# One transpose shared by two heads in the edge tiles of a neighbourhood attention

## The chip, the core and the metric

The kernel runs on one core of a Trainium2 chip. A core has five engines that work side by side, each through its own queue in order: TensorE (PE: matmuls and transposes), VectorE (DVE), ScalarE (ACT), GpSimd (POOL) and SyncE (SP, which here only issues transfers). SBUF is the on-chip memory with 128 partitions; PSUM holds the results of PE. The metric is the time of one execution on the device, in microseconds (us); smaller is better.

## What is computed

One layer of an encoder on 1024 tokens of width 1024, in float32: a projection, then a convolution group and an attention group side by side, an output projection, and a gated feed-forward block. The change concerns the attention alone: eight heads of width 64 on a grid of 16 rows by 64 columns, where each query sees a window of 8 rows by 16 columns, shifted inwards at the edges.

```python
def row_block(r):
    row_start = jnp.clip(r - kh // 2, 0, rows - kh)
    q_r = lax.dynamic_index_in_dim(qg, r, axis=1, keepdims=False)
    k_rows = lax.dynamic_slice_in_dim(kg, row_start, kh, axis=1)
    v_rows = lax.dynamic_slice_in_dim(vg, row_start, kh, axis=1)
    k_win = k_rows[:, :, col_idx]
    v_win = v_rows[:, :, col_idx]
    s = jnp.einsum("bqhd,brqchd->bhqrc", q_r, k_win) * scale
    ...
    s = s + jnp.transpose(bias, (0, 2, 1, 3))[None]
    p = jax.nn.softmax(s, axis=(-2, -1))
    return jnp.einsum("bhqrc,brqchd->bqhd", p.astype(v_win.dtype), v_win)
```

## The kernel before

The queries are cut into eight tiles of 128: `rh` is the upper or lower half of the grid rows, `cb` one of four blocks of 16 columns. A tile's keys are a rectangle: 11 or 12 grid rows (`AR`) by 23, 31, 31 or 24 grid columns (`WIN`). `order` takes the tiles as stages in the order cb = 0, 3, 1, 2, upper half before lower. The first four stages are those at the grid's left and right edge: stage 0, tile (0, 0), has 11 x 23 = 253 keys; stage 1, tile (1, 0), 12 x 23 = 276; stages 2 and 3, tiles (0, 3) and (1, 3), 12 x 24 = 288. Stages 4 to 7 have up to 12 x 31 = 372. Each stage has four head pairs, so there are 32 pairs, number `i`.

The instructions stand in the order in which the Python code is written (`manual_schedule`); each engine works its own queue in order, and waits by semaphores. The main loop runs i = 2 to 33; one turn of it is called a pass below. Pass i does, for PE: the two score matmuls of pair i (`score_mm`, tiles `s`), the transposes of pair i - 2 (`flip`, from `e` to the PSUM tile `p`), in odd passes up to 17 four transposes for the convolution (`conv_norm`, tile `y`), and the weighing of pair i - 3 (`weigh`, value matmuls into `o`). Between them DVE adds the bias table `tab` and finds the maximum, ACT takes the exponential (`score_exp`), POOL scales the row by its sum (`score_norm`), and ACT (second head, `hh` = 1) and DVE (first head) copy the transposed block from `p` into SBUF as `pT` (`flip_out`). There is one buffer for `p`, so the transposes of a pass wait for the copies of the pass before.

A pair's keys do not fit one transpose, whose result has at most 128 partitions. `parts` cuts them: 253 keys into two overlapping pieces of 125 and 128, all others by grid rows into three pieces of four rows, 92, 96 or 124 keys. A pair of stages 1 to 3 takes six transposes and six value matmuls, each of 128 output columns. In the weighing the first head goes to partitions 0 to 63 of `o`, the second to 64 to 127.

The values are written by `value_out` (ACT) to the tensor `vd` in device memory, one row of 512 floats per token with the heads in order, and read back by SP's queue in the windows that the stages need: `load_v00` for stage 0, `load_vw` for four grid rows of a column window, two of them in one SBUF tile `vw`. The bias tables are read by the same queue (`table`), and so are the weights of the output projection (`issue`). Loads and stores take eight semaphore lanes in turn, so that a load waits, besides for its data and buffer, for the one eight places ahead of it.

In the profile `p` is line 713, `pT` 718, `o` 730, `s` 682, `e` 695 (DVE), 697 (ACT) and 704 (POOL), `y` 831, `vs` 444 and its store 445, `vw` 644, `v00` 658 to 662, `tab` 632. `z` at lines 124 to 126 are matmuls of the projections before, `zt` their transposes.

Of the kernel before, what the change touches and what calls it, by code (L numbers as in the profile page):

```python
# [76 lines left out]
def build(ctx, tc, a):  # L77
# [569 lines left out]
    SPLIT = 125  # L647
    v00 = []

    def load_v00(j):  # L650
        if not v00:
            w = G("v00").rearrange("p (g d) -> p g d", d=512)
            v00.extend((w[:SPLIT, 0], w[:, 1]))
        src = vd.rearrange("(r c) d -> r c d", c=GW)
        ncol = WIN[0][1]
        r, c = divmod(SPLIT, ncol)
        if j == 0:
            nc.sync.dma_start(v00[0][:r * ncol], src[:r, :ncol, :])
            nc.sync.dma_start(v00[0][r * ncol:], src[r, :c, :])
        else:  # L660
            nc.sync.dma_start(v00[1][:ncol - c], src[r, c:ncol, :])
            nc.sync.dma_start(v00[1][ncol - c:], src[r + 1:AR[0][0], :ncol, :])

    def parts(rh, cb):
        m = 4 * WIN[cb][1]
        if rh == cb == 0:
            return [(0, P, v00[0]), (SPLIT, SPLIT + P, v00[1])]
        return [(g * m, g * m + m, vw[cb, rh + g]) for g in range(3)]

    k4 = kT.rearrange("p c (r w) -> p c r w", w=GW)  # L670
    order = [(rh, cb) for cb in (0, 3, 1, 2) for rh in range(2)]
    tab, es, pTs, os_, at, sums, pp = {}, {}, {}, {}, {}, {}, {}
# [14 lines left out]
    def score_exp(i, ss):  # L687
        s_, hp = divmod(i, 4)
        rh, cb = order[s_]
        n = AR[rh][KIND[cb]] * WIN[cb][1]  # L690
        e = es[i] = G(f"e{i}").rearrange("p (h n) -> p h n", h=2)[:, :, :n]
        rs = SM(f"rs{i}", 2)
        for hh in range(2):
            mx = SM(f"mx{i}{hh}", 1)
            dve.tensor_tensor_reduce(out=e[:, hh], in0=ss[hh], in1=tab[rh, cb][2 * hp + hh], scale=-1.0,  # L695
                                     scalar=3.0e38, op0=OP.add, op1=OP.min, accum_out=mx)
            act.activation(e[:, hh], e[:, hh], AF.Exp, bias=mx, scale=-1.0, accum_out=rs[:, hh:hh + 1])  # L697
        sums[i] = rs
# [7 lines left out]
    def flip(i):  # L706
        s_, hp = divmod(i, 4)
        cuts = parts(*order[s_])
        pp[i] = cv(f"p{i}")
        for hh in range(2):  # L710
            for g, (l, r, _) in enumerate(cuts):
                o = hh * 512 + g * P
                pe.transpose(pp[i][:r - l, o:o + P], es[i][:, hh, l:r], ident)  # L713
        pTs[i] = G(f"pT{i}").rearrange("p (n h q) -> p n h q", h=2, q=P)[:cuts[0][1], :len(cuts)]

    def flip_out(i, hh):
        m, n = pTs[i].shape[:2]
        (dve.tensor_copy, act.copy)[hh](pTs[i][:, :, hh], pp[i][:m, hh * 512:hh * 512 + n * P].rearrange(
            "p (n q) -> p n q", q=P))

    def weigh(i):
# [4 lines left out]
        cuts = parts(rh, cb)  # L726
        for g, (_, _, v) in enumerate(cuts):
            for hh in range(2):
                c = (2 * hp + hh) * HD
                pe.matmul(os_[s_][hh * HD:(hh + 1) * HD, hp], v[:, c:c + HD], pTs[i][:v.shape[0], g, hh],  # L730
                          start=g == 0, stop=g == len(cuts) - 1)
# [49 lines left out]
    for j in range(2):  # L781
        load_v00(j)
# [6 lines left out]
    for g in range(1, 4):  # L789
        load_vw(0, g)  # L790
    load_window(3)
# [648 lines left out]
```

## Time and profile before

| | |
|---|---|
| median of 3 runs | 1045.03 us (1044.88 to 1046.16) |
| the profiled execution | 1046.69 us, span of its instructions 1045.0 us |
| granted clock of PE | 0.997 |
| passes 2 to 18 of the loop | about 237 to 278 us of the span |

A profile is one execution. Its span runs from the first to the last instruction. All instants below are us from the span's start. A busy PE is not PE at its peak, since matmuls are pipelined and their ends are modelled; the chain of waits tells whether it is PE that everything waits for.

### The profile page before, as it was taken

What the parts mean: (1) busy time and instruction counts of PE and PEld (TensorE: products, weight loads), DVE (VectorE), ACT (ScalarE), POOL (GpSimd) and SP (SyncE); (2) the same over time, 40 slices, a digit from 0 to 9 for tenths busy, and PEclk for the clock granted to TensorE, in tenths of its full rate; (3) what the DMA queues carried; (4) which work ended last, traced back from release to release, by engine and by line L of the source; (5) the groups of instructions that cost most, each with busy time, mean ns of one, the idle gap of its engine ahead of it and who ended that gap; (6) DMA issues with size and microseconds to landing.
All of it is one profiled execution on the core that took longest, in us unless ns stands there. A gap on an engine that the chain in (4) does not pass through costs nothing.

```text
span 1045.0 us, 13870 instructions
## 1 busy us (share of the span) xinstructions
PE 1027.6 (98%) x4948; PEld 833.0 (80%) x4948; DVE 719.4 (69%) x1097; ACT 464.0 (44%) x915; POOL 451.9 (43%) x344
## 2 busy tenths in 40 slices
PE   7999999999999999999999999999999999999997
PEld 6888888876668888778888888888888888888886
DVE  6878998976885576876655655546556567768883
ACT  6465346627775676533232233232322443443441
POOL 0136668923574962754544454555454100002310
PEclk9999999999999999999999999999999999999999
DMA  9496871285546844555232232232232697634641
GB/s 355 169 261 232 211 226 64 78 241 180 158 106 156 171 170 148 123 143 186 84 131 101 73 132 98 99 123 101 91 111 81 212 328 254 204 101 130 212 131 41
DMA packets 73939, 162.44 MB, mean 155 GB/s; under 512 B 13533, under 2 KB 20445, under 8 KB 73166
## 3 DMA queue, kind: packets, MB, share of 16 engines
q1 hardware_dynamic: 67038, 143.64, 41.1%
q0 software_dynamic: 4864, 10.49, 6.2%
q10 hardware_dynamic: 1968, 7.42, 2.1%
q8 instruction: 39, 0.64, 0.2%
q14 instruction: 30, 0.25, 0.1%
HBM read 122.67 MB, written 52.71 MB: 168 GB/s over the span
## 4 chain that ended last, share of the span: by engine, by line
PE 91%; DVE 3%; ACT 2%; issue 2%; POOL 2%; DMA 1%; SPq 0%; POOLq 0%; ACTq 0%
PE B L125 5%; PE B L126 5%; PE B L124 5%; PE z L125 4%; PE z L124 4%; PE z L126 4%; PE D L126 4%; PE D L125 4%; PE D L124 4%; PE A L126 3%; PE A L125 3%; PE A L124 3%; PE gl L126 3%; PE gl L124 3%; PE gl L125 3%; PE n L124 3%
## 5 line engine op out<-in xcount | busy, mean ns | idle before, releaser
L358 DVE SCALAR_TENSOR_TENSOR cv<-u,par,cv 128x1009 f32<-128x1009 f32 (+14 forms) x85 | 108.5, 1276 | 1.9
L384 POOL TENSOR_TENSOR pa<-pa,pr 128x1022 f32<-128x1022 f32 (+10 forms) x31 | 75.5, 2435 | 33.2 <-ACT pr L383 32.3
L1395 POOL TENSOR_TENSOR ou<-ou,resm 128x512 f32<-128x512 f32 x8 | 12.8, 1608 | 141.3 <-DMA resm<-xd 140.7
L116 ACT CAST op<-sr 128x512 fp32r<-128x512 f32 x77 | 47.7, 619 | 53.0 <-PE B2d L126 22.1
L120 DVE TENSOR_TENSOR op<-sr,op 128x512 fp32r<-128x512 f32 x77 | 58.2, 756 | 15.8 <-ACT op L116 15.8
L1232 DVE TENSOR_TENSOR g<-B,g 128x512 f32<-128x512 f32 x22 | 15.2, 690 | 71.3 <-PE B L126 68.2
L1241 ACT ACTIVATE D<-D 128x512 f32<-128x512 f32 x22 | 12.8, 582 | 113.4 <-DVE D L1240 113.4
L1224 DVE TENSOR_TENSOR u<-B,g 128x512 f32<-128x512 f32 x22 | 15.2, 691 | 61.0 <-PE B L126 61.0
L116 ACT CAST op<-wd 128x512 fp32r<-128x512 f32 x66 | 40.9, 620 | 30.3 <-DVE wd L1319 17.1
L704 POOL TENSOR_SCALAR e<-e,rs 128x372 f32<-128x372 f32 (+3 forms) x64 | 34.6, 565 | 43.2 <-DVE rs L702 32.8
L120 DVE TENSOR_TENSOR op<-wd,op 128x512 fp32r<-128x512 f32 x66 | 51.4, 778 | 2.0 <-ACT op L116 0.3
L1025 DVE TENSOR_TENSOR ts<-ts,gu 128x512 f32<-128x512 f32 x36 | 43.3, 1203 | 0.6
L1230 ACT ACTIVATE A<-A 128x512 f32<-128x512 f32 x18 | 10.5, 582 | 68.6 <-PE A L126 68.6
L697 ACT ACTIVATE e<-e,mx 128x372 f32<-128x372 f32 (+3 forms) x64 | 35.6, 559 | 2.3 <-DVE mx L695 2.2
L695 DVE CUSTOM_DVE_ANT_0 e<-s,tab 128x372 f32<-128x372 f32 (+3 forms) x64 | 28.9, 489 | 8.6 <-PE s L682 8.1
L383 ACT ACTIVATE pr<-u,par 128x1022 f32<-128x1022 f32 (+10 forms) x31 | 34.2, 1135 | 1.2 <-ACT vs L444 1.2
L713 PEld LDWEIGHTS p<-ident,e 128*124 128x124 f32 (+3 forms) x184 | 19.2, 134 | 16.9 <-POOL e L704 9.6
L1025 DVE TENSOR_TENSOR ts<-gu 128x512 f32<-128x512 f32 x18 | 30.1, 1670 | 0.0
L903 DVE TENSOR_TENSOR x<-x,n 128x512 f32<-128x512 f32 x32 | 21.0, 681 | 13.1 <-PE n L126 13.1
L713 PE MATMUL p<-ident,e 128*124 128x128 f32 (+3 forms) x184 | 27.7, 281 | 1.7 <-POOL e L704 0.8
L682 PE MATMUL s<-kT,qT 64*128 64x372 f32 (+3 forms) x128 | 26.1, 485 | 0.0
L124 PE MATMUL B2d<-op 128*128 128x512 f32 x66 | 25.8, 391 | 0.0
(1070 smaller groups left out, 3524.0 us busy)
## 6 DMA issues: line engine op xcount, KB each, us to landing
sr<-sd SPq DMA_DIRECT2D x77, 256.0 KB
gu<-in_gu SPq DMA_DIRECT2D x36, 512.0 KB
sd<-sd SPq DMA_DIRECT2D x22, 512.0 KB
wd<-in_wd SPq DMA_DIRECT2D x44, 256.0 KB
sd<-g SPq DMA_DIRECT2D x33, 256.0 KB
x<-in_x SPq DMA_DIRECT2D x12, 512.0 KB
xd<-x SPq DMA_DIRECT2D x8, 512.0 KB
resm<-xd SPq DMA_DIRECT2D x16, 256.0 KB
```

What stands on the lines that cost most here:

```text
L116: act.copy(hi, src)
L120: eng.tensor_tensor(*[w[..., sl] for w in (lo, src, hi.bitcast(F32))], OP.subtract)
L124: pe.matmul(acc, lh, rh, start=start, stop=False, skip_group_check=True)
L125: pe.matmul(acc, lh, rl, start=False, stop=False, skip_group_check=True)
L126: pe.matmul(acc, ll, rh, start=False, stop=stop, skip_group_check=True)
L358: dve.scalar_tensor_tensor(acc[:, o], uc[:, i], dwk[:, c, t:t + 1], acc[:, o], OP.mult, OP.add)
L383: act.activation(pr[:, o], uc[:, i], AF.Copy, scale=dwk[:, c, t:t + 1])
L384: pool.tensor_tensor(pa[:, o], pa[:, o], pr[:, o], OP.add)
L697: act.activation(e[:, hh], e[:, hh], AF.Exp, bias=mx, scale=-1.0, accum_out=rs[:, hh:hh + 1])
L704: pool.tensor_scalar(es[i][:, hh], es[i][:, hh], rs[:, hh:hh + 1], 1.0, op0=OP.mult, op1=OP.mult)
L713: pe.transpose(pp[i][:r - l, o:o + P], es[i][:, hh, l:r], ident)
L1025: dve.tensor_tensor(lr(tsum[i, 1])[n - 3] if o is None else o, l, r, OP.add)
```

## The change

In stages 1 to 3 the first head's keys are cut as 128, then up to the last 32, then these 32; the second head's as the first 32, then the middle, then the last 128. The two pieces of 32 keys lie side by side in memory, since the two heads' scores now stand in `e` without a gap, and one transpose of 64 columns (`flip`, the branch `if left`) takes both. A pair has five transposes: four of 128 columns and the shared one. ACT and DVE copy two blocks each instead of three, and DVE copies the 64 x 128 block as well. `weigh` still has six matmuls; the last two contract 32 keys, one on partitions 0 to 31, the other on 32 to 63.

The pieces no longer are whole grid rows, and differ between the two heads. `load_edge` loads them by ranges of keys, for the four even and the four odd heads apart; for this `vd` now has the even heads in its first 256 columns and the odd ones in the last 256 (`value_out`). A range is one load for its whole grid rows and one for each part of a row, so an edge takes 14 loads into a tile `ve` and a short tile `vl`. The loads of stages 1 and 2 are issued ahead of the loop, in the place of the seven loads of `vw`, those of stage 3 in pass 4. Stage 0 keeps its cut (`load_corner`).

```diff
     def value_out(t, z):
         vs = ST(f"vs{t}")
-        act.activation(vs, z, AF.Copy, scale=r1[:, t:t + 1])
+        by_head = lambda w, order: w.rearrange(f"p ({order} d) -> p c h d", h=2, c=4)
+        act.activation(by_head(vs, "h c"), by_head(z, "c h"), AF.Copy, scale=r1[:, t:t + 1])
...
+    LEFT = 32
+    cuts = {}
+
+    def load_keys(dst, rh, cb, l, r, cols=slice(0, 512)):
+        c0, ncol = WIN[cb]
+        src = vd.rearrange("(r c) d -> r c d", c=GW)[4 * rh:, c0:c0 + ncol, cols]
+        at_ = l
+        while at_ < r:
+            row, c = divmod(at_, ncol)
+            n = (r - at_) // ncol if c == 0 else 0
+            end = at_ + n * ncol if n else min(r, (row + 1) * ncol)
+            nc.sync.dma_start(dst[at_ - l:end - l], src[row:row + n] if n else src[row, c:c + end - at_, :])
+            at_ = end
...
+    def load_edge(rh, cb):
+        n = AR[rh][KIND[cb]] * WIN[cb][1]
+        w = G(f"ve{rh}{cb}").rearrange("p (g d) -> p g d", d=512)
+        left = ST(f"vl{rh}{cb}")[:2 * LEFT, :256]
+        ends = ((0, P, n - LEFT), (LEFT, n - P, n))
+        for g in range(2):
+            for hh in range(2):
+                l, r = ends[hh][g:g + 2]
+                cols = slice(hh * 256, hh * 256 + 256)
+                load_keys(w[:r - l, g, cols], rh, cb, l, r, cols)
+        for hh, l in enumerate((n - LEFT, 0)):
+            load_keys(left[hh * LEFT:(hh + 1) * LEFT], rh, cb, l, l + LEFT, slice(hh * 256, hh * 256 + 256))
+        cuts[rh, cb] = [[(e[g], w[:e[g + 1] - e[g], g]) for g in range(2)] for e in ends], (n - LEFT, left)
...
-        e = es[i] = G(f"e{i}").rearrange("p (h n) -> p h n", h=2)[:, :, :n]
+        flat[i] = G(f"e{i}")[:, :2 * n]
+        e = es[i] = flat[i].rearrange("p (h n) -> p h n", h=2)
...
         for hh in range(2):
-            for g, (l, r, _) in enumerate(cuts):
+            some, left = parts(*order[s_], hh)
+            for g, (l, r, _) in enumerate(some):
                 o = hh * 512 + g * P
                 pe.transpose(pp[i][:r - l, o:o + P], es[i][:, hh, l:r], ident)
+        if left:
+            pe.transpose(pp[i][:2 * LEFT, 256:384], flat[i][:, left[0]:left[0] + 2 * LEFT], ident)
...
+        copy(pTs[i][:m, :n, hh], pp[i][:m, hh * 512:hh * 512 + n * P].rearrange("p (n q) -> p n q", q=P))
+        if left and hh == 0:
+            copy(pTs[i][:2 * LEFT, 2, 0], pp[i][:2 * LEFT, 256:384])
...
+                if left and g == 2:
+                    ks = slice(hh * LEFT, hh * LEFT + LEFT)
+                    l, r = left[1][ks, hp * HD:hp * HD + HD], pTs[i][ks, 2, 0]
+                else:
+                    v, c = both[hh][0][g][2], hh * 256 + hp * HD
+                    l, r = v[:, c:c + HD], pTs[i][:v.shape[0], g, hh]
+                pe.matmul(os_[s_][hh * HD:(hh + 1) * HD, hp], l, r, start=g == 0, stop=g == n - 1)
...
-    for g in range(1, 4):
-        load_vw(0, g)
-    load_window(3)
+    load_edge(1, 0)
+    load_edge(0, 3)
     tab[1, 3] = table(1, 2)
...
+        if i == 4:
+            load_edge(1, 3)
```

Three places in the queues show what stands where. The first is PE's queue in an odd pass, the seventh (the scores of pair 7, the transposes of pair 5, `y`, and the first weighing of stage 1). Before:

```order
L682 MATMUL s_2316<-kT,qT 128x276
L682 MATMUL s_2318<-kT,qT 128x276
L713 MATMUL p_2323<-ident,e_2255 92x128 x6
L831 MATMUL y_2341<-ident,u_557 128x128
L831 MATMUL y_2341<-ident,u_986 128x128
L831 MATMUL y_2341<-ident,u_1155 128x128
L831 MATMUL y_2341<-ident,u_1338 128x128
L730 MATMUL o_2351<-pT_2297,vw_2135 64x128 x2
L730 MATMUL o_2351<-pT_2297,vw_2137 64x128 x4
```

And after (here `s` is line 703, `p` 735, the shared transpose 737, `y` 862, `o` 764):

```order
L703 MATMUL s_2353<-kT,qT 128x276
L703 MATMUL s_2355<-kT,qT 128x276
L735 MATMUL p_2360<-ident,e_2292 128x128 x4
L737 MATMUL p_2360<-ident,e_2292 64x128
L862 MATMUL y_2378<-ident,u_557 128x128
L862 MATMUL y_2378<-ident,u_986 128x128
L862 MATMUL y_2378<-ident,u_1155 128x128
L862 MATMUL y_2378<-ident,u_1338 128x128
L764 MATMUL o_2388<-pT_2333,ve_2135 64x128 x4
L764 MATMUL o_2388<-pT_2333,vl_2136 64x128 x2
```

The single transpose of 64 rows has come to stand between those of 128 and `y`, and the last two value matmuls read `vl`. In an even pass `y` is missing, and `o` follows the shared transpose at once.

The second place is DVE's queue in the same pass. Before:

```order
L702 RECIPROCAL rs_2300<-rs_2300 128x2
L695 ISA e_2332,mx_2334<-s_2316,tab_1977 128x276
L695 ISA mx_2334 128x1
L695 ISA e_2332,mx_2337<-s_2318,tab_1977 128x276
L695 ISA mx_2337 128x1
L718 COPY pT_2330<-p_2323 92x3x128
L840 BN_STATS bs_2346<-y_2341 128x6
```

And after:

```order
L724 RECIPROCAL rs_2336<-rs_2336 128x2
L717 ISA e_2368,mx_2370<-s_2353,tab_1977 128x276
L717 ISA mx_2370 128x1
L717 ISA e_2368,mx_2373<-s_2355,tab_1977 128x276
L717 ISA mx_2373 128x1
L744 COPY pT_2366<-p_2360 128x2x128
L746 COPY pT_2366<-p_2360 64x128
L871 BN_STATS bs_2383<-y_2378 128x6
```

One copy of three blocks has become one of two blocks and one of the shared block.

The third place is SP's queue behind the loads of stage 0, with the semaphores that a row waits for (`DMAHW` with a number is one of the eight lanes of the loads, so a wait for it is one for an earlier load or store). Before, from the last two `vw` loads ahead of the loop:

```order
L644 DMA vw_2143<-vd 96x1x512 [waits DMAHW5_49,DVE_49]
L644 DMA vw_2143<-vd 96x1x512 [waits DMAHW6_49]
L632 DMA tab_2146<-tf_108 128x2304 [waits PE_49]
L160 DMA P30r<-in_w 128x1024 [waits DMAHW0_49]
L632 DMA tab_2239<-tf_104 128x2976 [waits PE_49]
L644 DMA vw_2277<-vd 124x1x512 [waits DMAHW2_49,PE_49,Pool_49]
```

And after, from the same table (`tab_2167`, for stage 3) to the middle of the third edge's loads; the table of stage 4 (`tab_2239` before, `tab_2276` after) comes eight rows later:

```order
L633 DMA tab_2167<-tf_108 128x2304 [waits DMAHW4_49,PE_49]
L160 DMA P30r<-in_w 128x1024 [waits DMAHW5_49]
L659 DMA ve_2233<-vd 120x1x256 [waits DMAHW6_49]
L659 DMA ve_2233<-vd 8x256 [waits DMAHW7_49]
L659 DMA ve_2233<-vd 16x256 [waits DMAHW0_49]
L659 DMA ve_2233<-vd 96x1x256 [waits DMAHW1_49]
L659 DMA ve_2233<-vd 16x256 [waits DMAHW2_49]
L659 DMA ve_2233<-vd 16x256 [waits DMAHW3_49]
L659 DMA ve_2233<-vd 96x1x256 [waits DMAHW4_49]
```

Between the two tables now stand the 14 loads of an edge, of which the seventh waits for the lane of the first table. Ahead of `tab_2167` stand 28 loads where seven stood.

More of the change, by code (lines that the diff above doesn't have):

```diff
@@ L665, in parts @@
+    def parts(rh, cb, hh):
         m = 4 * WIN[cb][1]
[L666 to L668 removed]
+        if (rh, cb) in cuts:
+            return [(l, l + P, v) for l, v in cuts[rh, cb][0][hh]], cuts[rh, cb][1]
+        return [(g * m, g * m + m, vw[cb, rh + g]) for g in range(3)], None
     k4 = kT.rearrange("p c (r w) -> p c r w", w=GW)
     order = [(rh, cb) for cb in (0, 3, 1, 2) for rh in range(2)]
+    flat = {}
@@ L780, in build @@
     value(6)
-    for j in range(2):
-        load_v00(j)
+    load_corner()
     score_exp(0, s0)
```

41 lines of the change are left out of this document (15 added, 26 removed).

## The prediction

> **What bounds the kernel now.** I read the page's engine row first, then the busy times of the stretch that the change touches, then the chain of waits through it, and last what the queue of SyncE (SP) and VectorE (DVE) do there.
>
> ```profile
> PE 1027.6 (98%) x4948; PEld 833.0 (80%) x4948; DVE 719.4 (69%) x1097; ACT 464.0 (44%) x915; POOL 451.9 (43%) x344
> 248.60:270.00 21.40, 21.40 (x210) 15.21 (x210) 17.09 (x66) 16.79 (x51) 9.39 (x19) 1.00 0.68 207
> 276.00:311.00 35.00, 33.76 (x296) 21.01 (x298) 30.28 (x109) 28.20 (x87) 26.27 (x42) 1.00 0.41 110
> ```
>
> The second and third rows are stretches (from:to, length, then PE, PEld, DVE, ACT, POOL busy, granted clock, DMA share, GB/s). In the first of them, which holds most of the edge stages, TensorE (PE) is busy for all of 21.40 us at a clock of 1.00. Busy is not the same as needed, so the chain of waits has the word (start, length, what; xN is the number of records, of which a plain fp32 matmul shows two and a transpose one):
>
> ```profile
> 202.09 0.44 PE zt L431 x4
> 202.53 0.23 PE z L124
> ...
> 224.34 0.63 PE s L682 x4
> 224.96 0.43 PE z L124
> 225.40 0.24 PE z L125
> ...
> 238.26 0.38 ACT pT L718
> 238.66 0.43 DVE pT L718
> ...
> 241.55 0.59 PE p L713 x4
> 242.14 0.59 PE o L730 x8
> ...
> 247.76 0.83 PE p L713 x6
> 248.59 0.44 PE y L831 x4
> 249.03 0.81 PE o L730 x12
> 249.83 0.68 PE s L682 x4
> 250.52 0.79 PE p L713 x6
> 251.31 0.81 PE o L730 x12
> ...
> 258.59 0.44 PE y L831 x4
> 259.03 0.81 PE o L730 x12
> 259.83 0.69 PE s L682 x4
> ...
> 269.84 0.82 PE s L682 x4
> ...
> 275.95 0.82 PE p L713 x6
> 276.79 0.48 ACT pT L718
> 277.27 1.18 ACT e L697 x4
> ```
>
> From 247.76 to 276.79 every piece of the chain is PE, each starting where the one before it ends. So here a microsecond of PE is a microsecond of the kernel; behind 276.79 the chain goes over ACT, DVE and POOL, started by a PE group, and hands any shift on.
>
> The same rows give two prices. Per item: p x4 takes 0.59 and p x6 0.79, o x8 (four matmuls) 0.59 and o x12 (six) 0.81, y x4 0.44. Each transpose and each 128-column matmul costs 0.10 to 0.11 us. Per group: 0.59 is not 4 x 0.11 but 0.15 more, in p and in o alike, while y, which follows p, costs 0.44 = 4 x 0.11 and nothing more. What differs is the part of the array used. The built program marks p, y and z as 128x128 (rows x columns), o as 128x64, s as 64x128. From p to y the part stays; p to o, o to s and s to p change it. The z rows say the same: after zt (128x128 too) z takes its usual 0.23, after s 0.43, that is 0.20 more. I read 0.15 to 0.20 us as the price of a change of the array's part, and take 0.15, the value of the two groups (p, o) that the change touches.
>
> **The change, part by part.** It concerns passes 6 to 18 of the attention loop: twelve head pairs of the three edge stages, six of them transposed in odd passes, where y stands behind p, and six in even ones, where o does.
>
> Removed: one transpose in each of twelve pairs, six becoming five. 12 x 0.11 = 1.3 us less on PE. The four full ones are 128 wide instead of 92 or 96; p x4 at 0.59 is that width already.
>
> Added on PE, changes of part. The shared transpose yields 64 rows, and the program marks it 128x64; the two last matmuls of each weighing contract 32 keys and are marked 32x64. In an even pass the order was s, p, o, s (three changes); now s, p, shared p, o, last o, s, where shared p and o have one part: four. In an odd pass it was s, p, y, o, s (three); now s, p, shared p, y, o, last o, s: six. Counting all matmuls of the built program gives 100 changes before and 124 after. 6 x 1 + 6 x 3 = 24, by 0.15 = 3.6 us more. The number of matmuls in a weighing stays at six, and I give the short ones the same 0.11: the two heads sit side by side in the array's columns already, so 32 rows make no new room. [...] Bounds for the changes: 24 x 0 = 0 if such short groups hide it, 24 x 0.20 = 4.8 by z behind s.
>
> Added on PE, semaphores. In the first weighing of each edge every matmul waits for its own loads, and PE's queue holds 20 more semaphore instructions than before (132 for 112).
>
> ```profile
> L713 PEldq EVENT_SEMAPHORE  x31: 51/51/51, 239.1 to 315.1; - x31
> L718 DVE COPY pT<-p 96x384 f32<-96x384 f32 x8 | 4.4, 554 | 2.2 <-ACT pT L718 2.2
> L718 ACT COPY pT<-p 96x384 f32<-96x384 f32 x8 | 3.8, 474 | 3.9 <-PE p L713 3.9
> L718 DVE COPY pT<-p 128x256 f32<-128x256 f32 x3 | 1.3, 423 | 0.1
> L718 ACT COPY pT<-p 128x256 f32<-128x256 f32 x3 | 1.1, 372 | 0.8 <-PE p L713 0.7
> ```
>
> At 51 ns they are 1.0 us at most and nothing at least, since the queue runs ahead of a 0.11 us matmul; I take 0.2.
>
> DVE and ACT. ACT's copy shrinks from 474 to 372 ns. DVE's goes from 554 to 423, and a 64x128 copy follows; by the slope (131 ns for 128 elements) it is 423 - 131 = 292. DVE gains 0.16 us per pair, 1.9 in all, against 21.40 - 17.09 = 4.3 us of free time in one stretch. Before the next p may overwrite the tile, the chain is ACT 0.37, DVE 0.42, DVE 0.29: 1.08 us, where it was 0.47 + 0.55 = 1.02. PE's time between two p of an even pass, o and s, is 0.81 + 0.69 = 1.5 and grows by a change of part. So it is covered, with 0.4 us to spare less hand-overs; were that cover gone, the 0.06 by twelve would be 0.7 us.
>
> value_out on ACT writes the same 512 columns in another order. Its store feeds loads that PE wants several us later (next part), so a slower write is hidden; its price is open, zero by its size.
>
> SP's queue. Seven loads become 42, in three groups of 14.
>
> ```profile
> 216.42 0.48 SPq L659 DMA_DIRECT2D v<-vd  x1
> 216.96 0.31 SPq L661 DMA_DIRECT2D v<-vd  x1
> 229.41 0.77 SPq L662 DMA_DIRECT2D v<-vd  x1
> 239.78 0.61 SPq L644 DMA_DIRECT2D vw<-vd  x1
> 243.25 0.56 SPq L632 DMA_DIRECT2D tab<-tf  x1
> 244.33 1.16 SPq L632 DMA_DIRECT2D tab<-tf  x1
> 245.60 17.00 SPq L644 DMA_DIRECT2D vw<-vd  x4
> 262.70 2.35 SPq L632 DMA_DIRECT2D tab<-tf  x1
> ```
>
> A 115-row load holds the queue 0.77, a 92-row one 0.61, one of 10 or 13 rows 0.31 to 0.48. A group of 14 is 2 x 0.8 + 2 x 0.6 + 10 x 0.35 = 6.3 us. The last value rows are there at 239.78 (the queue had waited for their store). Seven loads of the first edge are then left: 0.8 + 6 x 0.35 = 2.9, to 242.7, and PE wants them at 249.03. The second edge ends at 249.0, wanted at 259.03, its first weighing. The table of stage (1, 3) is then issued at 249 instead of 243.25 and wanted by DVE when s of 259.83 is done: 10 us for 1152 KB. The third edge, the next 6.3 us and some waiting, puts the table of stage 4 at about 258 instead of 244.33; it is wanted at s of 269.84, 11 us later, plus PE's own delay. The window loads behind it stood in the queue until 262.6 before, so from there the queue is level again. All of this lies beside PE: 0, with 1 to 4 us if a table is late.
>
> Sum against the profiled execution, span 1045.0, time 1046.69: -1.3 + 3.6 + 0.2 = +2.5 us, 1049.2. The three runs have a median of 1045.03, 1.66 below that execution; on their scale it is 1045.03 + 2.5 = **1047.5 us**, 0.24% slower.
>
> **Rivals.**
> (a) The change of part is not paid in groups of one or two records, because the array's latency covers it. For it: the price is known here only from groups of four or more. Against it: z after s pays it at once, in its first record. Then -1.3 + 0.2: 1043.9, not slower. It decides below 0.055 us per change (1.3 / 24).
> (b) The shared transpose runs on the full array after all. Then y and p stay together, only the change inside the weighing remains, 12 x 0.15 = 1.8, less 1.3, plus 0.2: +0.7, 1045.7. For it: the instruction only drops columns, as the 92-wide transposes did, which pay nothing before y. Against: the program's mark. [...] No row of the kernel before shows a 64-wide transpose, so the trace cannot say yet.
> (c) A table comes late. Eight loads may be under way on SP's queue (each waits for the load eight places ahead), so the third edge waits for the table and the weights in front of it. If that costs 6 us, the table of stage 4 is issued at 264, lands near 273, and DVE, ACT, POOL and PE of pass 16 stand for about 3.5 us: 1051.0. For it: that table is the last of a crowded queue and needs 1488 KB. Against: the margin of 11 us above, and DMA is 0.68 busy, not full.
> (d) The stage behind 276.79 gives some of it back, its waits being on ACT and POOL: half of 2.5 us, 1046.3. The chain hands over from PE to ACT at 276.79, which speaks against it.
>
> **How the numbers follow.** I give the forecast 0.55, (a) 0.15, (b) 0.13, (c) 0.10, (d) 0.07. The forecast's own range is 24 changes at 0.09 to 0.20 with semaphores 0 to 1.0: 1.3 less than 2.2 and 5.8, so 1045.9 to 1049.5. The range for all reaches to (a) below and a little past that above, 1043.8 to 1049.8; it leaves out (c) and a part of (a). A difference of 0.2% is 2.1 us, about what a measurement of this kernel tells from none. Of the forecast two thirds lie above it (0.37); with (c) and strays 0.49 is slower. Faster by as much needs more than the whole transpose saving: 0.06. The rest, 0.45, is the same.
>
> **What the profile after would show.** PE from the first edge transposes to pass 18 longer by 2 to 3 us; in odd passes a gap ahead of and behind the single shared transpose and ahead of the 32-key matmuls; p x4 still 0.59; no DVE row waiting for a table. Wrong: y starting 0.11 behind the shared transpose (b), the last o pair without a gap (a), or a tab wait near pass 12 or 16 (c).

## The result: 0.7% slower, and the profile after

| | before | after |
|---|---|---|
| median, six runs each | 1045.52 us (1044.88 to 1046.30) | 1053.00 us (1051.92 to 1054.75) |
| ratio | | 1.0072, 95% interval 1.0059 to 1.0084 |
| the profiled execution | 1046.69 us, span 1045.0 us | 1053.88 us, span 1052.2 us |

The loss is 7.5 us, where 2.5 were forecast and 1049.8 us was the end of the range. The engine row of the page hardly shows it (PE 1027.6 us busy before):

```profile
PE 1029.5 (98%) x4936; PEld 831.8 (79%) x4936; DVE 721.8 (69%) x1109; ACT 463.5 (44%) x915; POOL 451.6 (43%) x344
```

So the starts of the score matmuls `s` tell where the time went; each is read from the timeline of PE in both runs.

| score matmuls of pair | before | after | difference |
|---|---|---|---|
| 8 | 249.76 | 249.45 | -0.31 |
| 18 | 275.05 | 275.25 | +0.20 |
| 20 | 279.92 | 280.97 | +1.05 |
| 21 | 282.48 | 283.40 | +0.92 |
| 22 | 285.20 | 292.40 | +7.20 |
| 23 | 287.80 | 296.22 | +8.42 |
| 31 | 308.60 | 317.01 | +8.41 |

All of the edge stages, where the prediction looked for the loss, add half a microsecond. Six come in one step between pairs 21 and 22. (The span grows by 7.2, not 8.4: a run of the kernel before that is told below spent 1.0 us less behind the loop than the profiled one, so this part varies by itself. In the profiled one the granted clock fell to 0.50 once there, for 3.41 us from 448.86; in the other it didn't.)

First the half microsecond. The chain of waits in an odd and an even pass after:

```profile
247.44 0.58 PE p L735 x4
248.02 0.11 PE p L737
248.13 0.44 PE y L862 x4
248.57 0.95 PE o L764 x12
249.52 0.69 PE s L703 x4
250.21 0.58 PE p L735 x4
250.79 0.11 PE p L737
250.91 0.95 PE o L764 x12
```

The shared transpose (line 737) takes 0.11 right behind the full ones, and `y` takes its 0.44 right behind it, so no change of the array's part is paid on either side. The weighing takes 0.95 where it took 0.81.

Now the step of six. The chain of waits across it, and the timeline of PE (in brackets the idle time before an instruction, and what ended it):

```profile
267.23 14.99 DMA tab<-tf
...
282.29 5.42 issue
...
287.84 0.54 DVE e L717
```

```profile
280.60 0.44 PE L764 MATMUL o<-pT,vw 124*64 124x128 f32 x4 [0.48 <-DMA vw<-vd]
...
283.40 0.90 PE L703 MATMUL s<-kT,qT 64*128 64x372 f32 x4
289.48 1.51 PE L735 MATMUL p<-ident,e 128*124 128x128 f32 x6 [5.18 <-DVE rcq L885]
290.92 1.55 PE L764 MATMUL o<-pT,vw 124*64 124x128 f32 x12
292.40 1.61 PE L703 MATMUL s<-kT,qT 64*128 64x372 f32 x4
293.94 1.54 PE L735 MATMUL p<-ident,e 128*124 128x128 f32 x6
295.41 0.88 PE L764 MATMUL o<-pT,vw 124*64 124x128 f32 x12
296.22 0.90 PE L703 MATMUL s<-kT,qT 64*128 64x372 f32 x4
```

DVE stands from 282.3 to 287.8 before `e` of pair 20, the first of stage 5, and what it waits for is that stage's bias table, issued at 267.23. (The chain calls the last 5.42 us "issue", since no single event matches; the transfer ahead of it names the table. Its last landing in this trace is at 287.63.) The same `e` in the timeline of DVE before, without a wait:

```profile
282.01 0.53 DVE L695 CUSTOM_DVE_ANT_0 e<-s,tab 128x372 f32<-128x372 f32 x1
```

Behind that `e` on DVE stands the copy that frees the tile `p`, so PE stands too, for 5.18 us; the first weighing of stage 4 had already waited for its window `vw`. And when PE starts again, its groups take 1.5 to 1.6 us in place of 0.9 for four groups. The busy times of that stretch (length, then PE, PEld, DVE, ACT, POOL, granted clock, DMA share, GB/s) say why:

```profile
290.00:295.00 5.00, 5.00 (x26) 3.31 (x25) 3.44 (x15) 2.02 (x7) 3.66 (x6) 0.50 0.57 170
```

The granted clock is 0.50, where it was 1.00 at the same place before. Two of the four slow groups, the scores of pair 22 and the transposes behind them, make the step from +7.20 to +8.42: 1.2 us on top of the wait. The two ahead of them, of 1.51 and 1.55, are part of the step to +7.20, next to the wait of 5.18. In this trace the clock fell within the 5.18 us of idle time, at 288.55, and came back at 295.37, 5.9 us after PE had started again.

Why the table is late begins in SP's queue (start, time in the queue):

```profile
252.00 7.64 SPq L659 DMA_DIRECT2D ve<-vd  x10
259.74 1.52 SPq L659 DMA_DIRECT2D vl<-vd  x4
261.35 0.36 SPq L633 DMA_DIRECT2D tab<-tf  x1
261.75 5.38 SPq L645 DMA_DIRECT2D vw<-vd  x4
267.23 5.04 SPq L633 DMA_DIRECT2D tab<-tf  x1
```

The third edge's 14 loads take 9.3 us. Behind them come stage 4's table, the window for stages 4 and 5, and at 267.23 the table in question, which had been issued at 262.70 before. Three more rows count: the bytes moved, before and after, and the busy times of a stretch of the kernel before while that table was on its way.

```profile
DMA packets 73939, 162.44 MB, mean 155 GB/s; under 512 B 13533, under 2 KB 20445, under 8 KB 73166
```

```profile
DMA packets 75344, 162.84 MB, mean 155 GB/s; under 512 B 13893, under 2 KB 22509, under 8 KB 74570
```

```profile
274.00:285.00 11.00, 10.75 (x102) 6.94 (x101) 10.13 (x38) 9.41 (x27) 6.93 (x12) 1.00 0.26 96
```

The change moves 0.40 MB more: stages 2 and 3 used to share a set of four blocks, now each edge loads its own. And while the last of the table was on its way, the DMA engines were busy by a quarter only.

The landings recorded in the traces tell which part of the table is late. Behind its issue a load of four grid rows has four landings, a table 16. Of the table in question twelve come by 272.33 before and by 279.92 after. The last four come at 280.93 to 281.75 before and at 285.93 to 287.63 after, behind the last landing of the fourth window load (278.18 and 283.79).

### The profile page after: what moved, and what is told of

It is laid out like the page before. It is cut to its first block, busy times and chain, and to the rows that moved or that the text cites. A ratio compares the mean times of both kernels' runs of the same rounds, so it can differ in the third digit from the quotient of the medians.

```text
span 1052.2 us, 13934 instructions
## 1 busy us (share of the span) xinstructions
PE 1029.5 (98%) x4936; PEld 831.8 (79%) x4936; DVE 721.8 (69%) x1109; ACT 463.5 (44%) x915; POOL 451.6 (43%) x344
## 2 busy tenths in 40 slices
DMA packets 75344, 162.84 MB, mean 155 GB/s; under 512 B 13893, under 2 KB 22509, under 8 KB 74570
## 4 chain that ended last, share of the span: by engine, by line
PE 92%; DMA 2%; DVE 2%; issue 1%; POOL 1%; ACT 1%; SPq 0%; POOLq 0%; DVEq 0%; ACTq 0%
PE B L124 6%; PE B L125 6%; PE B L126 6%; PE z L125 4%; PE z L124 4%; PE z L126 4%; PE D L125 4%; PE A L124 4%; PE D L126 4%; PE A L125 4%; PE A L126 4%; PE D L124 4%; PE gl L124 3%; PE gl L125 3%; PE gl L126 3%; PE n L124 3%
## 5 line engine op out<-in xcount | busy, mean ns | idle before, releaser
L735 PEld LDWEIGHTS p<-ident,e 128*124 128x124 f32 (+1 forms) x160 | 17.9, 145 | 22.0 <-issue 13.5
L735 PE MATMUL p<-ident,e 128*124 128x128 f32 (+1 forms) x160 | 26.5, 295 | 6.5 <-DVE rcq L885 5.2
```

## The experiments

Theory P is the prediction's (changes of the array's part). All others start from the late table: T says that it is the loss. The other letters are guesses why it is late: the time that the 14 loads hold SP's queue (Q), their bytes (B, Y), their number (N), or four DMA engines that are full (W, F). C is about the clock. Each time is a median beside runs of the kernel before on the same chip, with the ratio to these.

### Order: the table ahead of the window

```diff
-        if i in (6, 18):
+        if i in (9, 18):
             load_window(1 + i // 18)
```

In the changed kernel:

> The changed kernel, with one edit: window 1 is loaded in pass 9, behind stage 5's bias table, where pass 6 loaded it ahead of that table. Computes the reference. Theory T (the loss is DVE's wait for stage 5's table, whose last pieces share four DMA engines with the window loads): the wait of 5.55 us ahead of e(20) goes, and with it PE's idle time of 5.2 us and the half clock behind it; what stays is the PE part, +0.5, and a wait of the first weighing of stage 4 for its window, 1 to 3 us: 1046.0 to 1049.0. Theory P (the prediction's: the changes of the array's part cost the time): nothing changes, 1052 to 1054.

And in the kernel before:

> The kernel before, with the same edit as the run above (window 1 loaded in pass 9, behind stage 5's table). Computes the reference. Theory T: the kernel before had no wait for that table, only 0.3 us to spare, so nothing is won; the window comes later, and may cost up to 2 us in the first weighing of stage 4: 1045.0 to 1047.0. It is the fair base for the run above: the difference of the two is the PE part, +0.5 by T, +2.5 by P (sum of the prediction).

The changed kernel took 1052.08 us (ratio 1.0061, 1.0047 to 1.0074), the kernel before 1045.58 (0.9996, 0.9988 to 1.0005). The first is outside T's range and inside P's. But P had said that nothing changes, and that isn't so: the table's wait is gone, and the timeline of PE shows about the same loss at the first weighing of stage 4.

```profile
279.40 0.44 PE L764 MATMUL o<-pT,vw 124*64 124x128 f32 x4 [0.46 <-DMA vw<-vd]
281.90 0.44 PE L764 MATMUL o<-pT,vw 124*64 124x128 f32 x4 [2.06 <-DMA vw<-vd]
284.41 0.69 PE L764 MATMUL o<-pT,vw 124*64 124x128 f32 x4 [2.06 <-DMA vw<-vd]
```

Each block of four grid rows (124 packets of 2 KB) comes 2.5 us after the one before. So the order only chooses who waits: table and window together are late. For the kernel before the order makes no difference. The two runs differ by 6.5 us, where T had 0.5 and P 2.5. One more thing this order shows: SP was through with the table at 264.1 here and at 272.27 in the changed kernel, so it was not the table's buffer that held the issue there.

### The loads without the change on PE

```diff
-        ends = ((0, P, n - LEFT), (LEFT, n - P, n))
...
+        blocks = [w[:m, 0], w[:m, 1], left[:m]]
...
+        cuts[rh, cb] = [[(g * m, blocks[g]) for g in range(3)]] * 2, None
```

> The changed kernel with its part on PE undone: each edge stage is again cut in three key blocks of 92 or 96 rows, six transposes and six weighings of full height per pair, no shared transpose; the loads stay three groups of 14 (in half heads), at the same places, of the same bytes. Computes the reference. Theory T: the loss is in SP's queue and stays: 1051 to 1053, with DVE waiting some 4 to 6 us for stage 5's table. Theory P: back at the kernel before, 1045 to 1046.5.

1057.04 us (1.0107, 1.0089 to 1.0126): the loss is in the loads, and P falls. (An edge takes 13 loads here, not 14, of the same bytes.) The loss is even larger than the change's, and past T's range; in the profiled run the table went out later still. From its chain of waits:

```profile
273.24 17.27 DMA tab<-tf
```


### PE kept busy during the wait

```diff
             ss = score_mm(i)
+            if i == 21:
+                for _ in range(44):
+                    pe.transpose(os_[4][:, 3], ident, ident)
```

> The changed kernel with 44 more transposes of the identity on PE (4.8 us of work nobody reads), put into the 5.2 us in which PE stood idle in pass 21 behind s(21). Computes the reference. Theory C (part of the loss is the granted clock, 0.50 for 290 to 295 us, behind that idle time): with PE kept busy the clock stays at 1.00, the groups of passes 21 and 22 take 0.87 instead of 1.55, and the kernel is faster than the changed one by 1 to 2 us, though it does more: 1051.0 to 1052.0. Rival (the slow groups hide behind DVE and ACT, which come out of the same wait): 1053 or slightly more, clock 1.00 or not.

1056.53 us (1.0101, 1.0087 to 1.0115), slower than the changed kernel, but it doesn't tell what was asked. In its profiled run the table was issued at 274.01, not 267.23, ahead of anything that the edit touches, and PE had stood 3.7 us for the window before. Why these transfers came later is open. Behind the filling the groups have the length that C said:

```profile
289.75 5.02 PE L985 MATMUL o<-ident 128*128 128x128 f32 x44
294.61 0.82 PE L735 MATMUL p<-ident,e 128*124 128x128 f32 x6
295.36 0.88 PE L764 MATMUL o<-pT,vw 124*64 124x128 f32 x12
```

0.82 and 0.88 instead of 1.5. But DVE was free again at 291.1, so that the filling itself stood in the way until 294.6.

### The third edge left out

```diff
         if i == 4:
-            load_edge(1, 3)
+            cuts[1, 3] = cuts[0, 3]
```

> The changed kernel without the 14 loads of its third edge; stage 3 is weighed with the values of stage 2's edge instead (wrong values, same work on every other engine). Everything of the change on PE, DVE and ACT stays. Theory Q (the 14 loads hold SP's queue some 9 us, so that the window's and stage 5's table's transfers start late and bunch up on the DMA engines): the window is issued near 252 and stage 5's table by about 264 as before; no wait for either, time 1045.5 to 1046.5, of which +0.5 is PE's. Theory W (it is the window loads' four DMA engines alone that are too slow, whenever they start): a wait of 2 us or more for window or table stays, 1048 to 1053.

1046.51 us (1.0007, 0.9997 to 1.0016), at the end of Q's range and below W's. Of the 7.5 us 0.9 is left. PE does all that it does in the changed kernel, and its score matmuls drift by +0.51 from pair 8 to pair 18, as they do there. SP:

```profile
252.46 2.77 SPq L645 DMA_DIRECT2D vw<-vd  x4
255.32 7.18 SPq L633 DMA_DIRECT2D tab<-tf  x1
```

This shows that the third edge's loads cost some 6.6 us, and PE's part about half a microsecond. What about them costs it is the next question. It isn't the table's issue alone: here the table went out at 255.32, 7.4 us earlier than in the kernel before, and its last landing is at 281.41, where it was 281.75.

### Each window load cut into rows

```diff
+        for r in range(4):
+            nc.sync.dma_start(vw[cb, g][r * ncol:(r + 1) * ncol], grid[g * 4 + r, c0:c0 + ncol, :])
```

> The changed kernel, with each window load of 4 grid rows cut into four loads of one row (16 for a window where there were 4). Computes the reference. [...] Theory Q: the queue is as late as before or later, with 12 more loads in it, so the table is no earlier: 1052 to 1056.

1110.68 us (1.0621, 1.0606 to 1.0635), far past Q's range. Theory W had this run faster than the changed kernel, on an estimate of the author's that a load of one row is spread over more DMA engines than one of four rows. The run shows the opposite. While PE waited for these loads, the busy times read

```profile
282.00:300.00 18.00, 1.13 (x8) 0.52 (x8) 0.00 (x0) 0.00 (x0) 1.16 (x3) 0.53 0.07 25
```

A DMA share of 0.07 is about one engine of 16, at 25 GB/s; with loads of four rows the row of the kernel before shows 0.26, about four of 16, at 96 GB/s. Which engines they are, no run here shows.

### The shared part on full tiles

```diff
-            pe.transpose(pp[i][:2 * LEFT, 256:384], flat[i][:, left[0]:left[0] + 2 * LEFT], ident)
+            pe.transpose(pp[i][:, 256:384], flat[i][:, left[0] - LEFT:left[0] - LEFT + P], ident)
...
-                    l, r = left[1][ks, hp * HD:hp * HD + HD], pTs[i][ks, 2, 0]
+                    l, r = left[1][:, c:c + HD], pTs[i][:, 2, 0]      # other keys' values are 0
```

> The changed kernel with its shared part on full tiles: the shared transpose is 128 columns wide, and the last two weighings of a pair contract 128 keys, of which the loaded values of 96 are zero (POOL clears the tile; three clears of 128x512). Computes the reference. The same number of matmuls and transposes, no 32-row part of the array. If a change of the array's part costs the 0.14 us per weighing (0.95 for 0.81), the weighing is back at 0.81 and the score groups of passes 5 to 18 drift by -1.3 us against the kernel before (12 transposes fewer) in place of +0.45. If the 0.14 us is the price of something else (the wait for its copy, the loads), the weighing stays at 0.95. The wait for table and window behind pass 18 stays: 1051 to 1054 by both, the group's time tells them apart.

1052.51 us (1.0069, 1.0057 to 1.0082). The chain of waits, even pass, then odd:

```profile
251.10 0.81 PE o L766 x12
...
253.18 0.11 PE p L739
253.29 0.44 PE y L864 x4
```

The weighing is back at 0.81, so 0.14 us is the price of going to the 32-row part. From pair 6 to pair 19 the score matmuls drift by -1.2 us against the kernel before: the twelve transposes saved. The time stays about where it was (1053.00 before this edit): the wait behind takes the saving.

### The third edge on ACT's queue

```diff
-            load_edge(1, 3)
+            load_edge(1, 3, nc.scalar)
```

> The changed kernel with the 14 loads of the third edge issued on ACT's queue in place of SP's, same place in the program. Computes the reference. Theory Q: SP's queue is free at 252, the window and stage 5's table go out 9 us earlier, and DVE does not wait for the table; but ACT now stands for what SP stood for ahead of these loads (loads in flight), up to 5 us near pass 4 to 7, of which its free time hides a part: 1046 to 1051. Theory W: the four engines are late all the same: 1051 to 1054.

1066.65 us in one run. ACT's next copy had to wait for all 14 loads to be issued, which themselves waited:

```profile
260.64 0.37 ACT L744 COPY pT<-p 128x256 f32<-128x256 f32 x1 [18.37 <-DMA ve<-vd]
```

The 5 us allowed for that were far too few. PE was then 20 us late, so that nothing can be read about the table.

### The third edge behind the window

```diff
-        if i == 4:
-            load_edge(1, 3)
...
             load_window(1 + i // 18)
+        if i == 6:
+            load_edge(1, 3)
```

> The changed kernel with one edit of order: the 14 loads of the third edge are issued in pass 6 behind window 1, where pass 4 issued them ahead of it. Computes the reference; nothing is left out, and the number of loads, transposes and matmuls is that of the changed kernel. Theory Q: the window goes out near 252 as in the run without the third edge, the 14 loads follow to about 263, stage 5's table about 263 to 266, as in the kernel before; the third edge is wanted at 270. No wait, 1045.5 to 1047.0 (with PE's +0.5). Theory B (what hurts is the bytes of these loads on the DMA engines, wherever they stand between 252 and 270): a wait of 2 us or more for the third edge, the window or the table stays, 1048 to 1053.

> The run above (third edge behind window 1) and the full tiles (128-wide shared transpose, last weighings over 128 keys with zeros) together. Computes the reference. If the table's lateness was the whole loss and the changes of part PE's, the saving of twelve transposes is left: about -1.2 us against the kernel before, 1044.0 to 1045.0. By theory B: 1047 to 1052.

1061.11 us (1.0146, 1.0130 to 1.0163), and 1058.87 with full tiles (1.0128, 1.0112 to 1.0144). Now the third edge waits, in SP's queue and on PE:

```profile
256.98 22.13 SPq L659 DMA_DIRECT2D ve<-vd  x10
```

```profile
278.35 0.66 PE L764 MATMUL o<-pT,ve 128*64 128x128 f32 x2 [8.94 <-DMA ve<-vd]
```

Q had put the end of these loads at 263; it is past 280. Both runs are slower than either theory allowed. In these runs whatever stood behind something else in this queue was late.

### Fewer loads of the same bytes

The third edge in 3 loads of four grid rows, the two others unchanged:

> The changed kernel with its third edge alone laid out as three blocks of 96 keys, loaded by 3 loads of four grid rows in place of 14, at the same place (pass 4) and of the same 576 KB; its four pairs are transposed in six and weighed at full height again, the first and second edge stay as changed. Computes the reference. Theory N (the number of loads counts: each of the 14 must wait for the load eight places ahead, behind a table of 1.1 to 1.5 MB): SP is through with the third edge some 2 to 4 us after 252 in place of 9, stage 5's table goes out by 264 and there is no wait, or under 1 us: 1045.5 to 1047.0. Theory B (bytes): the table is as late as in the changed kernel, 1050 to 1053.

```diff
+        blocks = [w[:m, 0], w[:m, 1], ST("vl13")[:m]]
+        for g in range(3):
+            load_keys(blocks[g], 1, 3, g * m, g * m + m)
```

All three edges cut at whole rows, 6 loads each, on full tiles:

> The changed kernel with its cut moved to whole grid rows: even heads take rows 0 to 4, 5 to 9 and share rows 10 and 11, odd heads take rows 2 to 6, 7 to 11 and share rows 0 and 1, so that each edge needs 6 loads in place of 14 (same bytes); the shared transpose is 92 or 96 wide, and the last weighings contract 92 or 96 keys, half of them zeros (POOL clears that tile). Five transposes and six weighing matmuls per pair as in the changed kernel, no 32-row part. Computes the reference. Theory N: no wait for the table or the window, and PE saves 1.2 us as in the run with full tiles: 1043.5 to 1045.0, faster than both kernels. Theory B: 1049 to 1053.

```diff
-        ends = ((0, P, n - LEFT), (LEFT, n - P, n))
+        k, m = 2 * ncol, 5 * ncol        # 5 + 5 + 2 grid rows, odd heads from the other end
```

1054.60 us (1.0085, 1.0072 to 1.0099) and 1053.31 (1.0072, 1.0060 to 1.0085). N falls: the number of loads isn't it. Both are a little past B's ranges, too (1053 at most). SP in the first of them:

```profile
252.48 1.31 SPq L659 DMA_DIRECT2D ve<-vd  x2
253.89 0.61 SPq L659 DMA_DIRECT2D vl<-vd  x1
...
255.64 13.69 SPq L645 DMA_DIRECT2D vw<-vd  x4
269.43 4.23 SPq L633 DMA_DIRECT2D tab<-tf  x1
```

The third edge is through in 2 us instead of 9, and then the four window loads hold the queue for 13.7 instead of 5.4, so the table goes out at 269.43. What the queue doesn't wait for at the edge it waits for at the window.

### The same bytes on 4 or on 16 DMA engines

Three more loads, 576 KB, in the kernel before, as four grid rows of 24 keys each, then as 96 neighbouring rows each:

```diff
+        if i == 4:
+            for g, dst in enumerate((w[:96, 0], w[:96, 1], ST("xl")[:96])):
+                nc.sync.dma_start(dst, SRC)
```

> The kernel before (no part of the change) with three more loads in pass 4, ahead of window 1: four grid rows of 24 keys each, 576 KB in all, into tiles nobody reads. It stands for what the third edge adds to the queue. Theory F (a load of four grid rows uses four of the 16 DMA engines; these four are full from about 250 on, and every further byte on them puts off the last pieces of stage 5's table): 3 x 24 packets of 0.084 us are 6.0 us more on each of the four; the table's wait is 4 to 8 us: 1049 to 1054. Theory Q (the number of instructions and waits in SP's queue): three loads are 2 us of queue: 1045.5 to 1047.

> The run above with the three extra loads taken from 96 neighbouring rows of the value array each: as many loads, as many bytes and packets (288 of 2 KB), at the same place, but each spread over 16 DMA engines. Theory F: 1.5 us more per engine, 0 to 2 us late: 1045.5 to 1048. Theory Y (bytes and loads count, wherever they go): as the run above, 1049 to 1054.

1060.65 us (1.0143, 1.0125 to 1.0161) and 1057.27 (1.0118, 1.0099 to 1.0137). Both are past every range. The comparison failed by its own doing: ACT soon needed the place of the tile that nobody reads, and waited for its load. But the chains of waits give the times from issue to landing, first with four grid rows, then with 96 neighbouring ones (16 engines for these is an estimate, from the 16 landings of a table's 128 rows):

```profile
244.46 19.00 DMA xv<-vd
```

```profile
245.07 15.82 DMA xv<-vd
```

A load of 192 KB took 16 to 19 us, with none of the change in the kernel. And in the kernel before as it stands the first window load, issued at 245.60, has its last landing at 265.94: so the transfers were backed up here before, too. The same comparison in the changed kernel, without that tile (base: the third edge in 3 loads):

```diff
-            load_keys(blocks[g], 1, 3, g * m, g * m + m)
+            nc.sync.dma_start(blocks[g], vd[256 + g * m:256 + g * m + m, :])
```

> The run with the third edge in three loads, with one edit: each of the three loads takes 96 neighbouring rows of the value array (wrong values for stage 3) in place of four grid rows of 24. As many loads, bytes, packets and matmuls, at the same place; only the number of DMA engines differs, 16 for 4. Theory F (four engines are full and put off table and window): 4.5 us less on each of the four, so the waits of 1.3 us for the window and of some 5 us for stage 5's table nearly go: 1046 to 1049, where the run with four rows took 1054.6. Theory Y (bytes, whatever the engines): 1053 to 1056.

1052.19 us (1.0066, 1.0051 to 1.0080) for 1054.60, between the two theories. The window's wait of 1.33 us is gone, PE's idle time for the table fell from 5.45 to

```profile
288.10 1.51 PE L743 MATMUL p<-ident,e 128*124 128x128 f32 x6 [4.56 <-DVE rcq L893]
```

So neighbouring rows in place of grid rows count, for about 2 us in the trace (the intervals of the two times overlap), but that is not the whole: some 5.5 us more go away when the loads do.

### The window spread over 16 engines

```diff
+            for l, n in ((0, 16), (16, 15)):
+                nc.sync.dma_start(vw[cb, g][r * ncol + l:r * ncol + l + n], grid[g * 4 + r, c0 + l:c0 + l + n, :])
```

> The kernel with 6 loads per edge and full tiles (the run with few loads), with two more edits: stage 5's table is issued ahead of window 1 (window in pass 9), and each window load of 4 rows by 31 keys is cut into eight of 16 and 15 keys, which spread over 16 and 15 DMA engines (32 loads per window in place of 4, about 13 us of SP's queue). Computes the reference. Theory F: no four engines are full any more, the table is there in time, the window lands by about 280, where it is wanted at 277 to 280: 1043.5 to 1047, at best 1.2 us ahead of the kernel before. If SP's queue is the limit instead, the window is 5 us late or more: 1050 to 1056.

1059.25 us (1.0131, 1.0115 to 1.0147), past even the last sentence's 1056. Its reason is there: with 32 loads per window SP became the limit, and the chain of waits runs over one issue of 0.4 us after the other. So this run doesn't tell whether the spreading helps.

### The third edge from POOL's queue

```diff
-            load_edge(1, 3)
+            load_edge(1, 3, pool)        # base: 6 loads per edge, full tiles
```

> The kernel with 6 loads per edge and full tiles, with the third edge's 6 loads issued on POOL's queue in place of SP's. Computes the reference. If a queue of POOL spreads its packets over other engines than SP's queue does, or no longer holds SP's, the table is in time and PE's saving shows: 1044 to 1046. If its packets go to the same four engines (theory F, where a queue changes nothing): 1052 to 1055.

1049.47 us (1.0031, 1.0021 to 1.0041), 3.8 less than from SP, and between the two forecasts. No wait for window or table is left; the loss is in one place, where POOL issues for 4 us and its next normalisation comes late. POOL's row, and the wait of PE that follows from it:

```profile
241.62 1.41 POOL L659 DMA_DIRECT2D ve<-vd  x2
```

```profile
246.14 0.88 PE L736 MATMUL p<-ident,e 128*128 128x128 f32 x4 [2.43 <-POOL e L727]
```

Then the same loads one per pass, and stage 5's table from POOL too:

```diff
+        if slow:
+            slow.pop(0)()                                  # one load of the third edge
+        elif i == 9:
+            tab[1, 1] = tab[1, 2] = table(1, 1, pool)
```

> The kernel with 6 loads per edge and full tiles, with the third edge's 6 loads issued by POOL one per pass (passes 3 to 8, behind its normalisation of that pass), and stage 5's table by POOL in pass 9; SP issues neither. Computes the reference. The run with all 6 on POOL in pass 4 lost 3.7 us in one place, where POOL's normalisation stood behind 4 us of issuing, and had no wait for table or window behind it. Theory L (the loss is that table and window are issued and landed late, and nothing else): with 0.66 us per pass in POOL's free 1.4 us the stall goes too, and PE's saving is left: 1044 to 1046, at or ahead of the kernel before. Theory F in its strict form (the same bytes on four full DMA engines land no earlier, whoever issues them): a wait for window or table of 2 us or more stays, 1048 to 1053.

1047.62 us (1.0023, 1.0014 to 1.0033): it doesn't beat the kernel before, as L had it, but 5.6 of the 7.5 us by which the same loads from SP were slower are gone, with as many bytes moved (162.84 MB for 162.83). No wait of 2 us for window or table is left, so strict F falls. The profiled run has a span of 1045.3, and shows what is late now, stage 3's table, still in SP's queue:

```profile
261.68 0.46 DVE L726 CUSTOM_DVE_ANT_0 e<-s,tab 128x288 f32<-128x288 f32 x1 [0.66 <-DMA tab<-tf]
```

That eats part of PE's 1.2 us. By pair 31 the scores of this execution are level with the kernel before (-0.03), so where the rest of the 1.9 us that are left is lost stays open. Between 250 and 260 the DMA engines, with these loads from SP (6 per edge) and from POOL:

```profile
250.00:260.00 10.00, 10.00 (x97) 6.89 (x98) 8.08 (x35) 7.36 (x24) 3.72 (x8) 1.00 0.58 194
```

```profile
250.00:260.00 10.00, 10.00 (x96) 6.92 (x96) 8.01 (x33) 7.58 (x25) 5.25 (x11) 1.00 0.99 312
```

From SP they were 58% busy while table and window stood in its queue; from POOL 99%. The engines had room, and SP's queue did not fill it.

## Why the prediction was right or wrong

**The sign** was right (slower), the size and the cause were not: 2.5 us on PE were forecast, half a microsecond is there.

**Twelve transposes less, -1.3:** right. With full tiles the drift over these passes is -1.2.

**24 changes of the part, +3.6:** mis-sized. The price of 0.15 is right where it is paid, 0.14 in each weighing, as the full tiles show. But it is paid 12 times. The sentence that failed is that the program's mark of 128x64 for the shared transpose makes it another part: the trace has it at 0.11 between `p` and `y` with nothing added, as rival (b) said. -1.3 + 12 x 0.14 = +0.4, where the score matmuls drift by 0.5 from pair 6 (-0.18) to pair 19 (+0.35); for the semaphores that leaves a tenth of a microsecond (0.2 were allowed). The 0.11 for each 32-row matmul was the author's estimate, and no row shows it by itself: the whole group took 0.95, where it took 0.81 with full ones.

**DVE, ACT and the store, nothing:** right. PE waits for neither copy in these passes; in the changed kernel it is busy for all of the 10.00 us from 250 to 260, and the chain of waits there is PE's alone.

**SP's queue, "all of this lies beside PE: 0":** the step that failed. The edges came in time, as worked out, though SP was through with the second at 251.0 and not at 249.0. The group of 14 was put at 6.3 us "and some waiting"; it was 9.3. Then stands the sentence "The window loads behind it stood in the queue until 262.6 before, so from there the queue is level again". It took an end that the loads themselves had set for a point that the queue always reaches. What held them there was transfers not yet done, as far as the runs tell, and transfers put in ahead of them hold them longer: to 267.2 here, to 269.4 with 3 loads in front. So stage 5's table went out 4.5 us later and DVE got it 5.8 us later than it began before. The margin of that table was never looked up: DVE's `e` began in the trace before without a wait, but the landings in the same trace have the table's last piece at 281.75, 0.26 us ahead of it. The 0.40 MB more were not counted either.

**Rival (c)** had the kind of cause, a table late in SP's queue, with a chance of 0.10. It named stage 4's table, which came in time, and 3.5 us; it was the next table, and the wait was 5.5 on DVE and 5.2 on PE, with the half clock behind it, which no step had.

**What stays open:** why a load that SP issues lands 16 to 20 us later here. The number of loads is not the cause, neighbouring rows in place of grid rows take about 2 us off, and the same bytes from another queue cost far less (1049.47 us from POOL, 1053.31 from SP). The landings point at the engines of the window loads, which have four landings each: the table's last four pieces came 6 to 9 us behind the twelve others, before and after, and with the table issued by POOL all 16 came between 264.64 and 266.29. Whether POOL's loads run on other engines or only don't stand in line behind SP's, no run tells apart.

## What to carry to other kernels

When transfers are added to a queue, follow the queue to the last consumer that stands behind them, and ask of each for the time between its transfer's landing and its use; a consumer that starts "without a wait" may have a margin of nothing. Read the landing and not the issue: without the third edge the table went out 7.4 us earlier and landed when it had before. A stretch in which a queue stands on transfers is not slack to be used up: what was put ahead of it here pushed its end from 262.6 to 267.2. And look at the share of the DMA engines that a load keeps busy before its bytes: loads of four grid rows kept 0.26 of the 16 busy here, and another issuing queue was worth more than fewer loads (3.8 us with the third edge from POOL, nothing with 6 loads per edge in place of 14, 1053.31 us for 1053.00).

## What the runs showed of the hardware that was not expected

- The share of busy DMA engines went with the shape of the loads: with four rows of 31 keys per load 0.26 of the 16 at 96 GB/s, with one row of 31 keys 0.07 at 25 GB/s.
- With the third edge and a table issued by POOL the DMA engines were 99% busy between 250 and 260, with all of it issued by SP 58%, and the loss fell from 7.5 to 1.9 us.
- The transpose of 64 columns showed no price of a change of the array's part (0.11 us, nothing around it); a weighing whose last pair has 32 rows took 0.14 us more than one with full ones (0.95 for 0.81).
- After 5.18 us of idle time PE ran its next four groups in 1.5 to 1.6 us in place of 0.9, at a granted clock of 0.50.
